# Running sums of Strassen–Winograd block products made by accumulating in a PSUM bank (SwiGLU of a two-layer encoder)

## The chip, the cores and the metric

One NeuronCore of one Trainium2 (trn2) chip. The metric is the device time of the kernel in microseconds (us): the median of three runs. Before the change it is 3169.98 us (3168.97 to 3172.48).

## What is computed

A trunk of two layers is run on two inputs, a prompt and a sample, each of 512 tokens with 1024 features. Each layer adds a self-attention, a cross-attention to a memory and a SwiGLU to the residual; a last RMS norm ends it. Cut to what matters here:

```python
D_MODEL, SEQ, DEPTH, D_FF = 1024, 512, 2, 2816

def swiglu(h, w_gu, w_down):
    g, u = jnp.split(h @ w_gu, 2, axis=-1)
    return (jax.nn.silu(g) * u) @ w_down

def trunk(x, mem, ...):
    for layer in range(DEPTH):
        x = x + mix(rms_norm(x, norm_mix[layer]))          # layer 0: GQA and differential attention, layer 1: MLA
        x = x + memory_cross_attn(rms_norm(x, norm_cross[layer]), ...)
        x = x + swiglu(rms_norm(x, norm_ffn[layer]), w_gu[layer], w_down[layer])
    return rms_norm(x, final_norm)
```

All data are fp32. The change touches only the two SwiGLUs.

## The kernel before

**Matmuls.** Activations lie transposed, features on the 128 partitions and the 512 tokens of one input along the row, so that a tile is 128x512. An fp32 product is made of three matmuls on values that are split into a high and a low part (`gemm_k`, L726 to L729): high by high (L727), high by low (L728), low by high (L729). L96 casts the high part on ACT and L97 subtracts it for the low part on DVE or POOL.

**Seven products instead of eight.** The SwiGLU treats the two inputs together. A pair of weight row blocks makes two block rows, the two inputs make two block columns, and the 2x2 block product is done by Strassen and Winograd's scheme with seven block products P1 to P7. With u2 = P1+P6 and u3 = u2+P7 the four blocks of the result are c11 = P1+P2, c12 = u2+P5+P3, c21 = u3+P4 and c22 = u3+P5. Column 1 is the prompt (b = 0), column 2 the sample (b = 1). c21 and c22 are the two inputs of the "up" half, c11 and c12 those of the gate half, in the first matrix multiply.

**Weight operands.** `lhs_ops` (L994 to L1028) loads two weight row blocks r0 and r1 (tiles `wr`, three buffers, DMAs of L998 and L999, issued by SP), splits r0 whole (tiles `wh`, `wl`, two buffers: products 1 and 2), makes four combinations (tiles `ws`, three buffers; on POOL in the first matrix multiply, on DVE in the second) and splits those: s1 is for product 5, s2 for 6, s4 for 3, s3 for 7, and r1's right half (`a`) for 4. Each of these five has one buffer. In the first matrix multiply a cast of ACT (L96) and a subtraction of DVE (L97) make each; the next pair of blocks is loaded when the combinations and subtractions that read the `wr` tile are through.

**Products and banks.** `product` (L1030 to L1039) takes its PSUM bank from a rotation pg, pss, pg, pt: three banks of pg, two of pss, two of pt (and one `pa` for small things). Each product starts its bank afresh, and each is taken out of it by one ACT copy or one DVE addition.

**gate_up** (L1124 to L1168) makes the first matrix multiply in 22 chunks, each 7 products of 12 matmuls. ACT copies P1 (L1131) and P5 (L1135) out; DVE adds P2, P6, P7, P3 and P4 to what there is (helper `tt`, so these have the line L506); POOL adds P5 to u2 and to u3, and DVE's addition of P3 reads u2 after POOL's addition. Then both columns are scaled by 1/rms (tiles R), ACT makes the SiLU (L1150), POOL multiplies, and the operands of the second multiply are formed and stored (L1159 to L1168). In the first chunk of a layer R[1] is still being made: `settle` sends a few 128x1 matmuls (L143) and a broadcast (L160) through PE between products.

**down** (L1170 to L1240) makes the second matrix multiply over four groups of k blocks (2, 3, 3, 3), in each over four row pairs q, in each over the seven products. The right operands (`u` tiles) are loaded, cast (L1205) and subtracted once in a group. Seven accumulators for each q, 28 tiles, keep the seven sums of products over the groups: in group 0 three begin as the residual and four as an ACT copy of the product (L1221), and all else is added by DVE. After the last group each q takes eight additions of accumulators (L1226 to L1235), three on POOL and five on DVE, and one more residual; then `new_x` stores it and forms the next layer's operands. In layer 1 `down_last` (L1242 to L1303) does the last group for the two columns in turn and makes the final norm.

**Order.** The program is recorded in the order of the code, and a scheduler that simulates a timeline then fixes the order of the instructions on each engine, for all engines apart. On the chip each engine executes its list in that order and waits at the head of the list. SP issues the DMAs of loads and stores in the same way.

Of the kernel before, what the change touches and what calls it, by code (L numbers as in the profile page):

```python
# [34 lines left out]
def trunk_kernel(ctx, tc, xt, memt, gains, lams, w_in0, w_out0, w_in1, w_uq, w_ukv, w_out1,  # L35
# [690 lines left out]
    def gemm_k(o, wh, wl, xh, xl, first, last):  # L726
        nc.tensor.matmul(o, lhsT=wh, rhs=xh, start=first, stop=False)  # L727
        nc.tensor.matmul(o, lhsT=wh, rhs=xl, start=False, stop=False)  # L728
        nc.tensor.matmul(o, lhsT=wl, rhs=xh, start=False, stop=last)  # L729
# [394 lines left out]
    def gate_up(l, gp, B, hd):  # L1124
        ctile = lambda: gp.tile([128, T], F32, tag="c", name=nm("c"), bufs=5)
        for c in range(NFF):
            A = lhs_ops(gp, w_gu[l, 2 * c], w_gu[l, 2 * c + 1], 512, nc.gpsimd if c else nc.vector, nc.vector)
# [3 lines left out]
            nc.scalar.copy(p1, product(1, A, B))  # L1131
# [342 lines left out]
```

## Time and profile before

| what | us |
|---|---|
| median of three runs | 3169.98 |
| the profiled execution | 3166.0 |
| its span | 3164.2 |
| PE busy in the span | 2967.1 |
| gate_up of layer 0 and its rim, about | 940 to 1404 |
| down of layer 0, about | 1404 to 1670 |
| gate_up of layer 1, about | 2400 to 2875 |
| down of layer 1, about | 2875 to 3136 |

The granted TensorE clock is 0.972 of full speed over the span. PE is TensorE's matmuls, PEld its weight loads, which overlap; DVE is VectorE, ACT ScalarE, POOL GpSimd, and SP issues DMAs. A group of the profile reads: line, engine, operation, output <- inputs, shape and count | busy us, mean ns of one | idle time just before them and what ended it. Windows of the span give the busy time and instruction count of each engine in a stretch.

### The profile page before, as it was taken

What the parts mean: (1) busy time and instruction counts of PE and PEld (TensorE: products, weight loads), DVE (VectorE), ACT (ScalarE), POOL (GpSimd) and SP (SyncE); (2) the same over time, 40 slices, a digit from 0 to 9 for tenths busy, and PEclk for the clock granted to TensorE, in tenths of its full rate; (3) what the DMA queues carried; (4) which work ended last, traced back from release to release, by engine and by line L of the source; (5) the groups of instructions that cost most, each with busy time, mean ns of one, the idle gap of its engine ahead of it and who ended that gap; (6) DMA issues with size and microseconds to landing.
All of it is one profiled execution on the core that took longest, in us unless ns stands there. A gap on an engine that the chain in (4) does not pass through costs nothing. (4 is left out here: it accounts for less than half of the span.)

```text
span 3164.2 us, 42343 instructions
## 1 busy us (share of the span) xinstructions
PE 2967.1 (94%) x14301; PEld 2438.6 (77%) x14301; DVE 2187.6 (69%) x3561; ACT 1348.0 (43%) x2554; POOL 1814.1 (57%) x1334
## 2 busy tenths in 40 slices
PE   8999999999988999988989899999997999998996
PEld 6878889878877877766767688888885888776774
DVE  7566676655587666677795566657569666668778
ACT  3255456535433232234442456656443322224432
POOL 4453445537576555657694333645667666556666
PEclk9999999999999999999999899999998999999998
DMA  4454653634342222244441777644442222225432
GB/s 145 165 172 141 217 190 131 203 103 167 123 143 74 100 100 94 97 149 149 150 148 56 238 256 242 209 148 147 147 157 90 97 95 96 91 99 190 157 128 81
DMA packets 204137, 449.70 MB, mean 142 GB/s; under 512 B 21264, under 2 KB 47248, under 8 KB 203920
## 3 DMA queue, kind: packets, MB, share of 16 engines
q1 hardware_dynamic: 203776, 446.95, 41.1%
q8 instruction: 114, 1.87, 0.2%
q14 instruction: 103, 0.84, 0.1%
q10 hardware_dynamic: 144, 0.04, 0.0%
HBM read 315.83 MB, written 131.07 MB: 141 GB/s over the span
## 5 line engine op out<-in xcount | busy, mean ns | idle before, releaser
L108 POOL TENSOR_TENSOR wl<-wr,wh 128x1024 fp32r<-128x1024 f32 (+1 forms) x160 | 396.9, 2482 | 317.5 <-ACT wh L107 312.4
L115 PE MATMUL pg<-u,wh 128*128 128x512 f32 x1360 | 546.0, 403 | 27.7 <-DVE acc L506 7.3
L117 PE MATMUL pg<-u,wl 128*128 128x512 f32 x1360 | 542.5, 399 | 11.1 <-POOL wl L108 10.8
L116 PE MATMUL pg<-u,wh 128*128 128x512 f32 x1360 | 544.4, 400 | 5.2 <-DVE u L231 4.8
L430 POOL TENSOR_SCALAR p<-p,rs 128x512 f32<-128x512 f32 (+1 forms) x288 | 194.3, 678 | 386.5 <-DVE rs L426 335.2
L115 PEld LDWEIGHTS pg<-u,wh 128*128 128x128 f32 x1360 | 260.7, 192 | 87.4 <-ACT wh L107 7.1
L117 PEld LDWEIGHTS pg<-u,wl 128*128 128x128 f32 x1360 | 260.6, 192 | 66.9 <-POOL wl L108 14.5
L116 PEld LDWEIGHTS pg<-u,wh 128*128 128x128 f32 x1360 | 260.7, 192 | 61.7 <-DVE u L231 10.9
L107 ACT CAST wh<-wr 128x1024 fp32r<-128x1024 f32 (+2 forms) x168 | 168.7, 1009 | 213.6 <-PE pg L116 146.6
L96 ACT CAST s<-ws 128x512 fp32r<-128x512 f32 (+2 forms) x304 | 165.9, 560 | 199.5 <-POOL ws L506 86.6
L727 PE MATMUL pg<-u,s 128*128 128x512 f32 x462 | 189.2, 409 | 45.9 <-DVE c L506 20.6
L425 ACT ACTIVATE p<-p,mx 128x512 f32<-128x512 f32 (+1 forms) x256 | 171.3, 670 | 102.8 <-DVE mx L422 95.3
L438 ACT CAST ptt<-pt 128x512 fp32r<-128x512 f32 (+1 forms) x288 | 151.3, 537 | 144.1 <-PE pt L436 141.2
L506 POOL TENSOR_TENSOR f<-f,c 128x512 f32<-128x512 f32 x132 | 174.2, 1321 | 63.7 <-DVE f L506 58.0
L439 DVE TENSOR_TENSOR ptt<-pt,ptt 128x512 fp32r<-128x512 f32 (+1 forms) x288 | 177.7, 624 | 40.9 <-ACT ptt L438 39.0
L1150 ACT ACTIVATE c<-c 128x512 f32<-128x512 f32 x88 | 55.7, 633 | 335.6 <-DVE c L506 335.5
L728 PE MATMUL pg<-u,s 128*128 128x512 f32 x462 | 188.0, 407 | 4.5 <-DVE u L506 4.4
L729 PE MATMUL pg<-u,s 128*128 128x512 f32 x462 | 187.7, 406 | 2.2 <-POOL s L97 2.2
L97 DVE TENSOR_TENSOR s<-ws,s 128x512 fp32r<-128x512 f32 x176 | 179.0, 1017 | 8.9 <-ACT s L96 6.8
L96 ACT CAST wh<-wr 128x1024 fp32r<-128x1024 f32 (+2 forms) x76 | 71.3, 938 | 253.2 <-DMA wr<-in_w_gu_dram 175.2
L226 POOL TENSOR_TENSOR ssq<-ssq,f 128x512 f32<-128x512 f32 x100 | 160.6, 1608 | 26.5 <-ACT f L224 26.2
L97 POOL TENSOR_TENSOR s<-ws,s 128x384 fp32r<-128x384 f32 (+1 forms) x128 | 149.3, 1176 | 38.5 <-ACT s L96 36.0
(368 smaller groups left out, 8187.2 us busy)
## 6 DMA issues: line engine op xcount, KB each, us to landing
dram<-hl SPq DMA_DIRECT2D x88, 512.0 KB, 3.1
wr<-in_w_gu_dram SPq DMA_DIRECT2D x88, 512.0 KB, 3.2
u<-dram SPq DMA_DIRECT2D x160, 256.0 KB, 4.8
dram<-f SPq DMA_DIRECT2D x152, 256.0 KB, 2.1
kk<-dram SPq DMA_DIRECT2D x52, 512.0 KB, 4.9
q<-dram SPq DMA_DIRECT2D x96, 256.0 KB, 4.1
vt<-dram SPq DMA_DIRECT2D x84, 256.0 KB, 3.1
wr<-in_w_down_dram SPq DMA_DIRECT2D x50, 384.0 KB, 3.0
```

The source lines that it names most:

```text
L96: nc.scalar.copy(hi, f)
L97: (eng or nc.vector).tensor_tensor(out=lo, in0=f, in1=raw(hi), op=SUB)
L108: (nc.vector if first else nc.gpsimd).tensor_tensor(out=l[:, cs], in0=r[:, cs], in1=raw(h[:, cs]), op=SUB)
L115: nc.tensor.matmul(ps, lhsT=wh, rhs=xh, start=(i == 0), stop=False)
L116: nc.tensor.matmul(ps, lhsT=wh, rhs=xl, start=False, stop=False)
L117: nc.tensor.matmul(ps, lhsT=wl, rhs=xh, start=False, stop=(i == n - 1))
L430: nc.gpsimd.tensor_scalar(out=p, in0=p, scalar1=rs, scalar2=1.0, op0=MUL, op1=MUL)
L439: nc.vector.tensor_tensor(out=pl, in0=tv, in1=raw(ph), op=SUB)
L506: eng.tensor_tensor(out=out, in0=a, in1=b, op=op)
L727: nc.tensor.matmul(o, lhsT=wh, rhs=xh, start=first, stop=False)
L728: nc.tensor.matmul(o, lhsT=wh, rhs=xl, start=False, stop=False)
L729: nc.tensor.matmul(o, lhsT=wl, rhs=xh, start=False, stop=last)
```

## The change

A product no longer owns a bank. A chunk (or a row pair) takes three banks: one of pg takes products 1, 6, 7, 4 one after the other, one of pss takes 5 and 3, one of pt takes 2. Only the first matmul into a bank starts it afresh; the products behind it accumulate on top. So the bank of pg shows P1, then P1+P6, then u3, then c21; whatever reads a running sum reads it between two products, and the next product into that bank waits for this reader.

In gate_up ACT copies out the bank after products 1, 6, 5 and 7 (L1144 to L1146 of the changed kernel: S1, S6, S5, S7). DVE makes c11 = P2+S1 and c12 = (P5+P3)+S6, and multiplies c21 by R[0] straight out of the bank. POOL makes c22 = S7+S5. For each chunk three DVE additions and one POOL addition are gone, and two ACT copies are new.

In down four accumulators for each q, 16 tiles, all begin as the residual (four loads for each q in group 0). DVE adds the bank to one of them after each product: after 1 and 2 to c11's, after 6 and 3 to c12's, after 4 to c21's, after 7 and 5 to c22's. For each layer the 16 ACT copies of group 0 become DVE additions, and the eight closing additions for each q (20 of DVE and 12 of POOL) and the six `u` tiles among the accumulators are gone. In layer 1 `sums` replaces the bodies of `first` and `second`.

```diff
-    def product(i, A, B):
-        ps = banks[bank[0] % 4]()
-        bank[0] += 1
+    def product(i, A, B, ps, first):
         n = len(B[i])
         for k in range(n):
             wh, wl = (x[:, k * 128:(k + 1) * 128] for x in A[i])
-            gemm_k(ps, wh, wl, *B[i][k], k == 0, k == n - 1)
+            gemm_k(ps, wh, wl, *B[i][k], first and k == 0, k == n - 1, skip_group_check=True)
         return ps
-    banks, bank = (pg, pss, pg, pt_), [0]
+    CHAIN = {1: 0, 6: 0, 7: 0, 4: 0, 5: 1, 3: 1, 2: 2}
+    class Banks:
+        def __init__(self, A, B):
+            self.A, self.B, self.ps = A, B, [None] * 3
+        def __call__(self, i):
+            j = CHAIN[i]
+            first = self.ps[j] is None
+            if first:
+                self.ps[j] = (pg, pss, pt_)[j]()
+            return product(i, self.A, self.B, self.ps[j], first)
...
-            u3 = up[1]
-            p1 = ctile()
-            nc.scalar.copy(p1, product(1, A, B))
-            g0 = ctile()
-            tt(nc.vector, g0, product(2, A, B), p1, ADD)
-            p5 = ctile()
-            nc.scalar.copy(p5, product(5, A, B))
-            settle(1, pa, rms[1], begin=True)
-            u2 = ctile()
-            tt(nc.vector, u2, product(6, A, B), p1, ADD)
-            tt(nc.vector, u3, product(7, A, B), u2, ADD)
-            settle(1, pa, rms[1])
-            tt(nc.gpsimd, u2, u2, p5, ADD)
-            g1 = ctile()
-            tt(nc.vector, g1, product(3, A, B), u2, ADD)
-            tt(nc.vector, up[0], product(4, A, B), u3, ADD)
-            tt(nc.vector, up[0], up[0], R[0], MUL)
-            tt(nc.gpsimd, u3, u3, p5, ADD)
-            tt(nc.gpsimd, up[1], u3, R[1], MUL)
-            for b, g in enumerate((g0, g1)):
-                tt(nc.vector, g, g, R[b], MUL)
-                nc.scalar.activation(g, g, AF.Silu)
-                tt(nc.gpsimd, up[b], up[b], g, MUL)
+            P, S, g = Banks(A, B), {}, [None, None]
+            def keep(i):
+                S[i] = ctile()
+                nc.scalar.copy(S[i], P(i))
+            def c11():
+                g[0] = ctile()
+                tt(nc.vector, g[0], P(2), S[1], ADD)
+            def c12():
+                tt(nc.vector, S[6], P(3), S[6], ADD)
+                g[1] = S[6]
+            def c21():
+                tt(nc.vector, up[0], P(4), R[0], MUL)
+            keep(1)
+            c11()
+            if c:
+                keep(6)
+                keep(5)
+                keep(7)
+                c12()
+            else:
+                keep(5)
+                settle(1, pa, rms[1], begin=True)
+                keep(6)
+                c12()
+                settle(1, pa, rms[1])
+                keep(7)
+            c21()
+            tt(nc.gpsimd, up[1], S[7], S[5], ADD)
+            tt(nc.gpsimd, up[1], up[1], R[1], MUL)
+            for b in range(2):
+                tt(nc.vector, g[b], g[b], R[b], MUL)
+                nc.scalar.activation(g[b], g[b], AF.Silu)
+                tt(nc.gpsimd, up[b], up[b], g[b], MUL)
...
-        spare = [u_tile(g_, k_, F32) for g_, k_ in (("B", 0), ("B", 4), (y, 4)) for _ in range(2)]
-        spare += tile_(gp, "c", 5) + tile_(f_p, "f", 5)[:1] + tile_(gp, "x", 8)
-        spare += tile_(f_p, "res", 1) + tile_(f_p, "of", 1) + tile_(f_p, "sh", 1)
-        spare += tile_(r_p, "ra", 1) + tile_(r_p, "r", 4)
-        for q in range(4):
-            acc.append(dict(zip((2, 3, 4, 1, 6, 5, 7), spare[7 * q:])))
+        tile_ = lambda p, t, n: [p.tile([128, T], F32, tag=t, name=nm("acc"), bufs=k)
+                                 for k in (n,) * min(n, 7)]
+        spare = tile_(r_p, "ra", 1) + tile_(r_p, "r", 4)[:2] + tile_(f_p, "f", 5)[:1]
+        spare += tile_(gp, "c", 5) + tile_(gp, "x", 8)
+        acc = [spare[4 * q:4 * q + 4] for q in range(4)]
+        into = {1: 0, 2: 0, 6: 1, 3: 1, 4: 2, 7: 3, 5: 3}
+        rows = lambda q: ((0, q), (1, q), (0, q + 4), (1, q + 4))
         for gi, c0 in enumerate((0, 4, 10, 16)):
             hk = 3 if gi else 2
-            order = (1, 2, 3, 5, 6, 7, 4) if gi else (1, 2, 5, 6, 3, 7, 4)
+            order = (1, 2, 6, 5, 7, 3, 4) if gi else (1, 2, 5, 6, 3, 7, 4)
...
-                    for i, b, m in ((2, 0, q), (3, 1, q), (4, 0, q + 4)):
-                        dma(a[i], res[b][m])
+                    for f, (b, m) in zip(a, rows(q)):
+                        dma(f, res[b][m])
+                P = Banks(A, B)
                 for i in order:
-                    ps = product(i, A, B)
-                    if gi == 0 and i in (1, 5, 6, 7):
-                        nc.scalar.copy(a[i], ps)
-                    else:
-                        tt(nc.vector, a[i], ps, a[i], ADD)
+                    f = a[into[i]]
+                    tt(nc.vector, f, P(i), f, ADD)
                 if not last:
                     continue
-                r22 = f_tile()
-                dma(r22, res[1][q + 4])
-                tt(nc.gpsimd, a[2], a[2], a[1], ADD)
-                tt(nc.vector, a[6], a[6], a[1], ADD)
-                tt(nc.vector, a[7], a[7], a[6], ADD)
-                tt(nc.gpsimd, a[3], a[3], a[5], ADD)
-                tt(nc.gpsimd, a[5], a[5], r22, ADD)
-                tt(nc.vector, a[3], a[3], a[6], ADD)
-                tt(nc.vector, a[4], a[4], a[7], ADD)
-                tt(nc.vector, a[5], a[5], a[7], ADD)
-                for b, m, i in ((0, q, 2), (1, q, 3), (0, q + 4, 4), (1, q + 4, 5)):
-                    out[b][m] = a[i]
-                    new_x(b, m, a[i], g_next, st[b], "AB"[b])
+                for f, (b, m) in zip(a, rows(q)):
+                    new_x(b, m, f, g_next, st[b], "AB"[b])
...
+        def sums(q, A, b, order):
+            P = Banks(A, B)
+            for i in order:
+                f = acc[q][into[i]]
+                tt(nc.vector, f, P(i), f, ADD)
+            for f, (b_, m) in zip(acc[q], rows(q)):
+                if b_ == b:
+                    st[b].add(f, nc.vector if q == 3 else None)
+                    outs[b].append((m, f))
+        first = lambda q, A: sums(q, A, 0, (1, 2, 6, 7, 4))
+        second = lambda q, A: sums(q, A, 1, (5, 3))
```

The places where the order of instructions moves, with buffer numbers in the names. First PE in the first chunk of layer 0's gate_up, before; `pa` and L143 are `settle`, and the `pg` behind it is product 5:

```order
L728 MATMUL pss_10155<-u_9529,wh_10105 128x512
L729 MATMUL pss_10155<-u_9528,wl_10106 128x512
L143 MATMUL pa_10184<-cols,ssq_9652 128x1 x4
L727 MATMUL pg_10170<-u_9659,s_10111 128x512
L728 MATMUL pg_10170<-u_9660,s_10111 128x512
L729 MATMUL pg_10170<-u_9659,s_10112 128x512
L727 MATMUL pg_10170<-x_9804,s_10111 128x512
```

The same place on PE after the change; `pg_10320` and `pt_10335` are products 1 and 2 of the second chunk:

```order
L729 MATMUL pt_10155<-u_9528,wl_10106 128x512
L727 MATMUL pg_10320<-u_9141,wh_10285 128x512
L728 MATMUL pg_10320<-u_9142,wh_10285 128x512
L727 MATMUL pt_10335<-u_9390,wh_10285 128x512
L728 MATMUL pt_10335<-u_9391,wh_10285 128x512
L143 MATMUL pa_10184<-cols,ssq_9652 128x1 x4
L729 MATMUL pg_10320<-u_9141,wl_10286 128x512
L727 MATMUL pg_10320<-u_9226,wh_10285 128x512
L728 MATMUL pg_10320<-u_9227,wh_10285 128x512
```

24 matmuls of the second chunk's products 1 and 2 have moved ahead of product 5 of the first chunk, some of them ahead of the small matmuls.

ACT over one chunk of gate_up, before; L1131 and L1135 are the copies of P1 and P5, `wh` is the cast of a newly loaded weight tile, L1150 the SiLU:

```order
L1131 COPY c_10957<-pt_10958 128x512
L96 CAST wh_11239<-wr_11235 128x1024
L1150 ACTIVATE c_10972<-c_10972 128x512
L96 CAST s_11090<-ws_11088 128x512
L1135 COPY c_10987<-pss_10988 128x512
L96 CAST s_11096<-ws_11094 128x512
L96 CAST s_11108<-ws_11106 128x512
L96 CAST s_11102<-ws_11100 128x512
L1150 ACTIVATE c_11032<-c_11032 128x512
L96 CAST a_11112<-wr_11081 128x512
```

ACT over one chunk after the change; L1146 is a copy out of a running sum (first S6, then S5, S7, and S1 of the next chunk), L1178 the SiLU:

```order
L96 CAST a_10772<-wr_10741 128x512
L96 CAST wh_11048<-wr_11044 128x1024
L96 CAST s_10905<-ws_10903 128x512
L1146 COPY c_10808<-pg_10779 128x512
L1146 COPY c_10822<-pss_10823 128x512
L1178 ACTIVATE c_10793<-c_10793 128x512
L96 CAST s_11054<-ws_11052 128x512
L96 CAST s_10917<-ws_10915 128x512
L1146 COPY c_10837<-pg_10779 128x512
L1146 COPY c_10927<-pg_10928 128x512
L96 CAST s_10911<-ws_10909 128x512
L1178 ACTIVATE c_10808<-c_10808 128x512
```

The cast of `wh` now stands three places ahead of the copy of S6, and there are four copies in place of two.

DVE over one chunk of gate_up, before; `c<-pss` is the addition of P3, `f<-pg` those of P7 and P4:

```order
L97 TENSOR_TENSOR s_11562<-ws_11559,s_11561 128x512
L506 TENSOR_TENSOR c_11479<-pt_11480,c_11434 128x512
L97 TENSOR_TENSOR s_11568<-ws_11565,s_11567 128x512
L506 TENSOR_TENSOR f_11433<-pg_11494,c_11479 128x512
L97 TENSOR_TENSOR s_11580<-ws_11577,s_11579 128x512
L506 TENSOR_TENSOR c_11509<-pss_11510,c_11479 128x512
L97 TENSOR_TENSOR s_11574<-ws_11571,s_11573 128x512
L506 TENSOR_TENSOR c_11509<-c_11509,r_10242 128x512
L506 TENSOR_TENSOR f_11432<-pg_11524,f_11433 128x512
L97 TENSOR_TENSOR a_11584<-wr_11552,a_11583 128x512
L506 TENSOR_TENSOR f_11432<-f_11432,r_9757 128x512
L506 TENSOR_TENSOR c_11604<-pg_11605,c_11589 128x512
```

DVE over one chunk after the change; `f<-pg` with `r` is c21 by R[0], `c<-pt` is c11 and `c<-pss` c12:

```order
L506 TENSOR_TENSOR f_10776<-pg_10779,r_9757 128x512
L97 TENSOR_TENSOR a_10922<-wr_10890,a_10921 128x512
L506 TENSOR_TENSOR c_10942<-pt_10943,c_10927 128x512
L97 TENSOR_TENSOR wl_11198<-wr_11193,wh_11197 128x1024
L506 TENSOR_TENSOR c_10942<-c_10942,r_9757 128x512
L97 TENSOR_TENSOR s_11061<-ws_11058,s_11060 128x512
L506 TENSOR_TENSOR t_10885<-f_10777,f_10776 128x512
L97 TENSOR_TENSOR s_11204<-ws_11201,s_11203 128x512
L97 TENSOR_TENSOR s_11073<-ws_11070,s_11072 128x512
L506 TENSOR_TENSOR c_10957<-pss_10972,c_10957 128x512
L97 TENSOR_TENSOR s_11067<-ws_11064,s_11066 128x512
L506 TENSOR_TENSOR c_10957<-c_10957,r_10240 128x512
```

Three reads of banks are left of five, and none of them has an input that POOL makes.

More of the change, by code (lines that the diff above doesn't have):

```diff
@@ L724, in attn_diff, with gemm_k @@
             new_o(of, grp, os_)
[L726 to L729, printed above, removed]
+    def gemm_k(o, wh, wl, xh, xl, first, last, **k):
+        nc.tensor.matmul(o, lhsT=wh, rhs=xh, start=first, stop=False, **k)
+        nc.tensor.matmul(o, lhsT=wh, rhs=xl, start=False, stop=False, **k)
+        nc.tensor.matmul(o, lhsT=wl, rhs=xh, start=False, stop=last, **k)
     sqn = [[dram([128, 2, T]) for _ in range(8)] for _ in range(2)]
@@ L1170, in down @@
     def down(l, gp, x, y, hd, g_next):
-        out = [[None] * KC, [None] * KC]
-        acc = []
         st = [Stats(), Stats()]
-        tile_ = lambda p, t, n: [p.tile([128, T], F32, tag=t, name=nm("acc"), bufs=n)
-                                 for _ in range(n)]
-        spare = [u_tile(g_, k_, F32) for g_, k_ in (("B", 0), ("B", 4), (y, 4)) for _ in range(2)]
-        spare += tile_(gp, "c", 5) + tile_(f_p, "f", 5)[:1] + tile_(gp, "x", 8)
-        spare += tile_(f_p, "res", 1) + tile_(f_p, "of", 1) + tile_(f_p, "sh", 1)
-        spare += tile_(r_p, "ra", 1) + tile_(r_p, "r", 4)
-        for q in range(4):
-            acc.append(dict(zip((2, 3, 4, 1, 6, 5, 7), spare[7 * q:])))
+        tile_ = lambda p, t, n: [p.tile([128, T], F32, tag=t, name=nm("acc"), bufs=k)
[5 more added lines that the diff above has]
+        rows = lambda q: ((0, q), (1, q), (0, q + 4), (1, q + 4))
         for gi, c0 in enumerate((0, 4, 10, 16)):
             hk = 3 if gi else 2
-            order = (1, 2, 3, 5, 6, 7, 4) if gi else (1, 2, 5, 6, 3, 7, 4)
+            order = (1, 2, 6, 5, 7, 3, 4) if gi else (1, 2, 5, 6, 3, 7, 4)
             last = gi == 3
@@ L1207, in down @@
             if last and g_next is None:
-                return down_last(l, gp, B, acc, st)
+                return down_last(l, gp, B, acc, into, rows, st)
             for q in range(4):
@@ L1257, in down_last @@
         outs = [[], []]
-        def add_to(i, q, A):
-            tt(nc.vector, acc[q][i], product(i, A, B), acc[q][i], ADD)
-        def first(q, A):
-            a = acc[q]
-            r22 = f_tile()
-            dma(r22, res[1][q + 4])
-            for i in (1, 2, 6, 7, 4):
-                add_to(i, q, A)
-            tt(nc.vector, a[2], a[2], a[1], ADD)
-            tt(nc.vector, a[6], a[6], a[1], ADD)
-            tt(nc.vector, a[7], a[7], a[6], ADD)
-            tt(nc.vector, a[4], a[4], a[7], ADD)
-            for m, i in ((q, 2), (q + 4, 4)):
-                st[0].add(a[i], nc.vector if q == 3 else None)
-                outs[0].append((m, a[i]))
-            tt(nc.gpsimd, a[7], a[7], r22, ADD)
-            tt(nc.gpsimd, a[3], a[3], a[6], ADD)
-        def second(q, A):
-            a = acc[q]
-            add_to(5, q, A)
-            tt(nc.vector, a[3], a[3], a[5], ADD)
-            tt(nc.vector, a[5], a[5], a[7], ADD)
-            add_to(3, q, A)
-            for m, i in ((q + 4, 5), (q, 3)):
-                st[1].add(a[i], nc.vector if q == 3 else None)
-                outs[1].append((m, a[i]))
+        def sums(q, A, b, order):
[9 more added lines that the diff above has]
+        second = lambda q, A: sums(q, A, 1, (5, 3))
         ops = lambda q, *want: lhs_ops(gp, *src(q), nc.vector, nc.gpsimd, *want)
```

2 lines of the change are left out of this document (1 added, 1 removed).

## The prediction

> **What bounds the kernel now.** I read the page first: which engine is full, and over the whole span. The two lines are the span and the busy times of the engines.
>
> ```profile
> span 3164.2 us, 42343 instructions
> PE 2967.1 (94%) x14301; PEld 2438.6 (77%) x14301; DVE 2187.6 (69%) x3561; ACT 1348.0 (43%) x2554; POOL 1814.1 (57%) x1334
> ```
>
> PE is busy for 94%, and the change removes no matmul. All it can win is PE's idle time in the two SwiGLUs, or the rim of the span. So the next view is the windows, stage by stage: length, then busy time and instructions of PE, PEld, DVE, ACT and POOL, granted clock, DMA share, GB/s.
>
> ```profile
> 940.00:964.00 24.00, 11.03 (x40) 8.59 (x38) 23.93 (x27) 10.37 (x16) 18.70 (x11) 0.75 0.14 51
> 964.00:1160.00 196.00, 196.00 (x839) 158.44 (x840) 131.74 (x162) 59.03 (x99) 116.47 (x86) 0.99 0.26 95
> 1160.00:1404.00 244.00, 233.13 (x998) 186.09 (x998) 162.24 (x195) 70.31 (x120) 143.63 (x106) 1.00 0.27 98
> 2446.00:2700.00 254.00, 253.35 (x1097) 204.88 (x1096) 171.44 (x200) 75.28 (x126) 155.92 (x114) 1.00 0.27 97
> 2700.00:2875.00 175.00, 168.18 (x714) 134.30 (x713) 116.89 (x139) 50.27 (x86) 102.90 (x77) 0.99 0.27 95
> 1404.00:1500.00 96.00, 79.52 (x309) 59.50 (x309) 76.47 (x93) 45.60 (x93) 65.82 (x53) 0.95 0.52 183
> 1500.00:1600.00 100.00, 95.63 (x404) 75.60 (x403) 78.49 (x98) 44.66 (x81) 63.73 (x48) 0.98 0.46 158
> 1600.00:1652.00 52.00, 47.61 (x194) 36.99 (x192) 48.54 (x48) 20.18 (x35) 52.00 (x35) 0.96 0.36 119
> 1652.00:1670.00 18.00, 13.18 (x36) 8.97 (x37) 18.00 (x18) 4.33 (x7) 14.93 (x9) 0.69 0.33 117
> 2875.00:2970.00 95.00, 80.44 (x300) 59.74 (x300) 74.59 (x91) 45.97 (x93) 67.10 (x54) 0.91 0.53 185
> 2970.00:3070.00 100.00, 95.80 (x404) 76.24 (x402) 72.37 (x92) 42.83 (x77) 61.14 (x47) 0.98 0.48 162
> 3070.00:3136.00 66.00, 55.90 (x228) 42.04 (x227) 60.95 (x69) 17.90 (x33) 54.59 (x38) 0.97 0.12 43
> ```
>
> The second row has no idle time at all: 196 / 839 = 0.2336 us per matmul, so a chunk of 84 matmuls can't go below 19.6 us. Here PE is the bound. In the rows behind it, a few per cent are idle; around group 0 of down (from 1404 and 2875) it is 15 to 17%. What ends these waits is in PE's rows of the timeline (start, length, engine, line, tiles, and in brackets the idle time and its releaser), two out of each gate_up and two of down, with the two starts ahead of them:
>
> ```profile
> 963.87 0.79 PE L727 MATMUL pg<-u,s 128*128 128x512 f32 x1 [9.70 <-ACT s L96]
> 2438.34 0.80 PE L727 MATMUL pg<-u,s 128*128 128x512 f32 x1 [10.32 <-ACT s L96]
> 1168.09 0.47 PE L727 MATMUL pg<-u,s 128*128 128x512 f32 x1 [1.16 <-DVE c L506]
> 1372.43 0.47 PE L727 MATMUL pg<-u,s 128*128 128x512 f32 x1 [2.00 <-DVE c L506]
> 1475.59 0.50 PE L728 MATMUL pss<-u,s 128*128 128x512 f32 x1 [3.05 <-DVE u L506]
> 2890.44 0.65 PE L728 MATMUL pt<-u,s 128*128 128x512 f32 x1 [3.21 <-DVE u L506]
> ```
>
> Between the third and fourth row lie ten chunks: (1372.43 - 1168.09) / 10 = 20.43 us for each, 0.8 us over the floor. PE waits for a bank that DVE hasn't emptied, and DVE in turn waits, as the groups of 1000 to 1390 us show (busy, mean ns | idle before, releaser):
>
> ```profile
> L506 DVE TENSOR_TENSOR c<-pg,c 128x512 f32<-128x512 f32 x28 | 19.2, 685 | 43.4 <-POOL c L506 43.4
> L506 DVE TENSOR_TENSOR c<-pt,c 128x512 f32<-128x512 f32 x15 | 10.3, 684 | 5.9 <-POOL c L506 5.9
> L506 POOL TENSOR_TENSOR c<-c,c 128x512 f32<-128x512 f32 x19 | 27.1, 1428 | 11.7 <-ACT s L96 11.7
> ```
>
> DVE's addition of P3 stands behind POOL's u2 + P5 (1.43 us, at the end of a queue of combinations). That is the one link of gate_up in which work, not PE, sets the time.
>
> **The change in gate_up.** This link goes: P5 + P3 is summed in the bank, and no read of a bank has an input of POOL's. DVE loses three additions of 0.685 us, POOL one of 1.43 us, and ACT gains two copies, a duration that the DMA fence below shows as 0.58 us. None is full (DVE 67%, ACT 30%, POOL 59% of 1160 to 1404), so the counts themselves cost or win nothing; the link does. PE idles 244.00 - 233.13 = 10.9 us there, 0.65 in 2446 to 2700 and 6.8 in 2700 to 2875, together 18.3. I take 15.5 and leave 2.8 for new waits; bounds 0 (the ring of weights keeps the pace, rival A) and 18.3. That the new waits are small is a choice: between two products of one bank the order puts other work, 24 matmuls between 6 and 7 and between 7 and 4, or 24 x 0.2336 = 5.6 us in which the reader must finish.
>
> The start: PE stands still for 9.70 and 10.32 us in front of product 5 of the first chunk. There 24 matmuls of the second chunk now come first, 5.6 us. Less 2 us for new short waits (the broadcast of the norm now stands right behind product 6), 3.6 for each layer, 7.2 in all; bounds 0 and 11.2.
>
> **The change in down.** In group 0 sixteen ACT copies become DVE additions. The first row prices them; the other two show what the merging of accumulators costs in 1400 to 1660 us.
>
> ```profile
> L506 DVE TENSOR_TENSOR acc<-pg,acc 128x512 f32<-128x512 f32 x32 | 21.8, 680 | 2.7 <-PE pg L729 2.5
> L506 DVE TENSOR_TENSOR acc<-acc,acc 128x512 f32<-128x512 f32 x10 | 15.5, 1559 | 0.2
> L506 POOL TENSOR_TENSOR acc<-acc,acc 128x512 f32<-128x512 f32 x5 | 7.2, 1446 | 0.0
> ```
>
> 16 x 0.68 = 10.9 us more on a DVE that is busy 80% there (76.47 of 96) and that PE waits for (the last two rows of the timeline). Against that, down's products 1 and 2 of q = 0 now stand ahead of product 7 of chunk 20, the next group's first products stand in the group before, and six of the accumulators no longer occupy operand tiles. Fully exposed it costs 2 x 10.9 = 22; at best it wins most of the idle 16.5 + 14.6 = 31, say 28. I take a gain of 6, a little above the middle, since DVE's idle third of late gate_up lies next to it.
>
> Groups 1 to 3 up to the last few: PE idles 4.4 + 4.4 and 4.2 + 10.1 = 23 us. Where the last group ends, DVE is 93% and POOL 100% busy (1600 to 1652), and the closing additions, 20 x 1.56 = 31 us of DVE and 12 x 1.45 = 17 us of POOL a layer, leave it. DVE's share spreads over four q, most of it covered by PE. I take 10; bounds 0 and 19. The way out of layer 0 (1652 to 1670) has DVE at 18.00 of 18.00 and PE idle for 4.8 at a clock of 0.69: I take 4, bounds 0 and 8.
>
> The end: the last matmul is followed by the last additions and the norm.
>
> ```profile
> 3135.29 0.39 PE L729 MATMUL pt<-u,s 128*128 128x512 f32 x1
> 3137.54 0.68 DVE L506 TENSOR_TENSOR acc<-pt,acc 128x512 f32<-128x512 f32 x1
> 3138.14 0.15 DVE L123 TENSOR_SCALAR v<-pa 128x4 f32<-128x4 f32 x1
> ```
>
> The last product ends at 3135.68 and is taken up only at 3137.54, since DVE is still merging. 1.86 us can go; I take 1.3, bounds 0 and 1.9. The four residual loads for each q (before three, and one later) are hoisted into gate_up, where the DMAs are busy a quarter of the time: nothing.
>
> Sum: 15.5 + 7.2 + 6 + 10 + 4 + 1.3 = 44. From the profiled execution's 3166.0 this is 3122; the median of the runs is 4 higher, so 3169.98 - 44 = 3126.
>
> **Rivals.** A: the weight ring holds gate_up. Without PE the timeline of one chunk shows the ring's turn:
>
> ```profile
> 1108.70 0.61 ACT L96 CAST a<-wr 128x512 fp32r<-128x512 f32 x1
> 1109.21 0.58 ACT L1131 COPY c<-pss 128x512 f32<-128x512 f32 x1
> 1109.34 1.70 DVE L97 TENSOR_TENSOR a<-wr,a 128x512 fp32r<-128x512 f32 x1 [0.67 <-ACT a L96]
> 1111.06 0.33 SPq L998 DMA_DIRECT2D wr<-in_w_gu_dram  x1
> 1114.21 1.05 ACT L96 CAST wh<-wr 128x1024 fp32r<-128x1024 f32 x1 [4.42 <-DMA wr<-in_w_gu_dram]
> ```
>
> The subtraction that reads r1 ends at 1111.04, the load is sent at 1111.06, and ACT waits for it until 1114.21: 5.5 us from cast to cast. If this turn, and not POOL's addition, makes the 20.43 us, gate_up keeps its idle time: 3126 + 15.5 = 3142. Against it: the recorded wait is POOL's, 43.4 us of DVE; for it: the loads now wait for combinations of POOL's that have moved.
>
> B: group 0 is bound by DVE at full price, -22 in place of +6: 3126 + 28 = 3154. For it are the rows of waits for `u`; against it the slack on both sides.
>
> C, the slow side: the links show. In a chain the next product of a bank may not begin until the copy is out, and ACT runs in order. The copy of S6 now stands behind the cast of `wh`, which waits for a DMA. The cover is 5.6 us from product 6 to 7; with 0.58 for the copy the cast must end within 5.0 us behind product 6. If it ends later, PE stops, and the stop delays the operands that release the next load, so it comes again in each chunk: 44 us for each us late. With all four reads of a chunk exposed, 4 x 0.58 x 44 chunks = 102 us and nothing won in gate_up: 3126 + 15.5 + 102 = 3244. For it is the row of 4.42 us above; against it, by the order I reckon the cast done about 4 us ahead of need.
>
> The row of 0.58 us beside a cover of 5.6 says that the reader hides. [...]
>
> D: the additions were hidden anyway and nothing moves: 3170.
>
> **How the numbers follow.** Forecast 0.66, A 0.13, B 0.09, C 0.10, D 0.02. The predicted time is the forecast's, 3126. With every gain at its upper bound, 18.3 + 11.2 + 28 + 19 + 8 + 1.9 = 86, it would be 3084; all at once is unlikely, so the low end is 3090. The high end takes in A and B: 3156. About 0.2% of the time, 6.3 us, can be told from no change. Faster: the forecast, A, and 0.05 of B, which by its price lies 16 us below the time before, 0.84. Same: the other 0.04 of B, should A's loss come on top, and D, 0.06. Slower: C, 0.10.
>
> **What would show it.** Right: a gate_up without idle time, 19.6 us a chunk; no wait of DVE for POOL ahead of a read of a bank; about 4 to 6 us of stop at the start; fewer waits for `u` about group 0; the last group with DVE under 90%; the last addition right behind the last matmul. Wrong: PE waiting for the copies of L1146 (C), or for `wh` or its low part (A), or a longer stretch of group 0 with DVE full (B).

## The result and the profile after

The changed kernel takes 3087.8 us (median of four runs, 3084.74 to 3092.32) beside 3171.23 for the kernel before (3168.97 to 3176.46): a ratio of 0.9739, 95% interval 0.9723 to 0.9755. The forecast was 3126, range 3090 to 3156. The direction is right, the gain of 83 us is almost twice the 44 forecast, and the time lies 2 us under the range.

The page of the changed kernel, as before: span, then busy time, share and instructions of each engine.

```profile
span 3083.0 us, 41876 instructions
PE 2942.8 (95%) x14301; PEld 2429.3 (79%) x14301; DVE 2065.6 (67%) x3417; ACT 1391.7 (45%) x2610; POOL 1785.5 (58%) x1270
```

PE executes the same 14301 matmuls; the span is 81.2 us shorter, but its busy time also falls by 24 us. Where the 81.2 us lie can be counted without windows of fixed times: each layer's SwiGLU has 2772 matmuls, and it is cut alike in both traces behind the first 168 (two chunks), 1764 (21 chunks), 2016 (end of group 0 of down), 2268 and 2520 of them and at the start of the last one. Times in us, both layers summed:

| stretch | before | after | gain | forecast |
|---|---|---|---|---|
| start, two chunks | 118.0 | 104.6 | 13.4 | 7.2 |
| steady gate_up, 19 chunks | 759.1 | 740.4 | 18.7 | 15.5 |
| chunk 21 to the end of group 0 | 153.3 | 136.0 | 17.3 | 6 |
| groups 1 and 2 | 258.2 | 247.9 | 10.3 | 10 (groups 1 to 3) |
| group 3 | 146.7 | 128.8 | 17.9 | |
| layer 0's end to layer 1's gate_up | 758.7 | 754.3 | 4.4 | 4 |
| last matmul to the end | 28.9 | 29.3 | -0.4 | 1.3 |

(The stretch ahead of the first gate_up is 0.4 longer.) Now the windows that show these stretches after; columns as in the prediction.

```profile
994.00:1364.00 370.00, 370.00 (x1597) 299.07 (x1596) 230.65 (x252) 143.08 (x236) 241.23 (x153) 1.00 0.29 106
1364.00:1432.00 68.00, 62.46 (x255) 47.62 (x254) 64.59 (x85) 31.32 (x64) 49.24 (x40) 0.97 0.67 228
1432.00:1556.00 124.00, 120.50 (x507) 96.32 (x506) 89.26 (x120) 48.21 (x87) 77.84 (x60) 0.97 0.42 136
1556.00:1624.00 68.00, 63.86 (x268) 51.06 (x267) 52.97 (x60) 33.05 (x60) 55.33 (x40) 0.97 0.45 154
2431.00:2801.00 370.00, 370.00 (x1597) 299.07 (x1596) 232.90 (x252) 143.43 (x236) 241.81 (x153) 1.00 0.30 106
2994.00:3054.00 60.00, 58.81 (x251) 46.50 (x249) 38.53 (x50) 21.42 (x41) 42.42 (x34) 1.00 0.22 70
```

Steady gate_up has no idle time in either layer, and a chunk takes 370.2 / 19 = 19.5 us. DVE's share of the last group of layer 1 is 64% (38.53 of 60). Only the way into down (second row) is still tight: DVE 64.59 of 68.

The reads of the banks in the changed gate_up, groups of 1000 to 1390 us (busy, mean ns | idle before, releaser):

```profile
L1146 ACT COPY c<-pg 128x512 f32<-128x512 f32 x61 | 33.5, 583 | 0.0
L506 DVE TENSOR_TENSOR c<-pss,c 128x512 f32<-128x512 f32 x20 | 13.8, 691 | 29.3 <-PE pss L729 29.3
L506 DVE TENSOR_TENSOR f<-pg,r 128x512 f32<-128x512 f32 x20 | 13.8, 690 | 58.1 <-PE pg L729 58.1
L727 PE MATMUL pg<-u,a 128*128 128x512 f32 x61 | 24.2, 397 | 0.6 <-ACT c L1146 0.6
```

DVE now waits for PE and no longer for POOL. The last row answers the fear of rival C: PE waits once, 0.6 us, for an ACT copy between two products of a bank, and in the whole run there is no other such wait. In down the links do show, over the whole run:

```profile
PE pg L727 <- DVE acc L506: 11.8, 12, 2.8
PE pss L727 <- DVE acc L506: 2.0, 2, 1.6
```

### The profile page after: what moved, and what is told of

Same layout as the page of the kernel before. It is cut to its first block, busy times and chain, and to the rows that moved or that the text cites. A ratio compares the mean times of both kernels' runs of the same rounds, so it can differ in the third digit from the quotient of the medians.

```text
span 3083.0 us, 41876 instructions
## 1 busy us (share of the span) xinstructions
PE 2942.8 (95%) x14301; PEld 2429.3 (79%) x14301; DVE 2065.6 (67%) x3417; ACT 1391.7 (45%) x2610; POOL 1785.5 (58%) x1270
## 5 line engine op out<-in xcount | busy, mean ns | idle before, releaser
L107 ACT CAST wh<-wr 128x1024 fp32r<-128x1024 f32 (+2 forms) x168 | 168.7, 1009 | 214.9 <-PE pg L116 145.8
L727 PE MATMUL pss<-u,s 128*128 128x512 f32 x484 | 192.2, 398 | 7.2 <-ACT s L96 4.6
L506 POOL TENSOR_TENSOR f<-f,c 128x512 f32<-128x512 f32 x88 | 149.1, 1695 | 79.0 <-DVE f L506 75.8
L729 PE MATMUL pss<-u,s 128*128 128x512 f32 x484 | 192.3, 397 | 0.7 <-DVE s L97 0.7
L728 PE MATMUL pss<-u,s 128*128 128x512 f32 x484 | 192.1, 397 | 0.0
L727 PE MATMUL pg<-u,s 128*128 128x512 f32 x440 | 175.5, 399 | 5.0 <-DVE acc L506 2.7
L728 PE MATMUL pg<-u,s 128*128 128x512 f32 x440 | 174.5, 397 | 2.0 <-DVE u L506 2.0
```

Of the source, the lines that this page charges most:

```text
L729: nc.tensor.matmul(o, lhsT=wl, rhs=xh, start=False, stop=last, **k)
```

## The experiments

Theory at the outset: the parts of the gain belong to the places where the table has them, and in gate_up the wait of DVE for POOL is the cause. Rivals: the gain about group 0 comes out of gate_up; the wait only stands in the record, and the number of bank reads or the way in which the banks are shared matters. Each kernel was timed beside the one before on the same chip.

**One half alone.** The changed gate_up with the old down, and the old gate_up with the changed down; only whole functions are exchanged.

> The changed gate_up with the down of before (seven accumulators, rotating banks). Counted from the trace, the gain of 81 us in the span is 18.6 in steady gate_up, 13.5 at its start, 17.4 from chunk 21 to the end of group 0, 28 in groups 1 to 3 and 4.4 on the way out of layer 0. Theory 1, the parts add up and each belongs to its own function: 32 us of 81, so about 3139 beside 3171 for before. Theory 2, the gain about group 0 comes from gate_up's banks, which let down's first products start early: 32 + 17 = 49 us, about 3122.

> The gate_up of before with the changed down (four accumulators, banks that accumulate). Theory 1: 17.4 + 28 + 4.4 = 50 us gained, about 3121. Theory 2, the gain about group 0 needs the changed gate_up: 32 us, about 3139. Rival B of the prediction, sixteen more DVE additions in group 0 cost about 10 us a layer and the gain there comes from elsewhere: about 3130 or more.

Measured 3117.86 (ratio 0.9824, 0.9800 to 0.9849) and 3140.54 (0.9902, 0.9882 to 0.9922), beside 3171.11. gate_up alone gives 53 us, down alone 31, and 53 + 31 = 84 is the whole: the halves add up. But the cut is theory 2's. With the changed gate_up alone the stretch into down takes 63.4 and 63.2 us (before 76.6 and 76.7); with the changed down alone 76.5 and 80.8. What I had put down to down is gate_up's.

**One word.** In the kernel before, DVE in place of POOL adds P5 to u2:

```diff
-            tt(nc.gpsimd, u2, u2, p5, ADD)
+            tt(nc.vector, u2, u2, p5, ADD)
```

> Before, with one word changed: u2 + P5 is added by DVE and not by POOL. No accumulation in a bank. Theory: DVE's wait for POOL ahead of P3 makes steady gate_up slow, so its 18 us go and the rest stays: 3153, with chunks of 19.5 us. Rival: it is the number of bank reads, or the weight ring behind them, and the wait for POOL only stands in the record: chunks stay at 20.4 us and the time within 5 us of 3171, or above, since DVE has 0.7 to 1.6 us more to do in a chunk.

Measured 3124.22 (0.9855, 0.9835 to 0.9874): 47 us, where 18 were expected. Steady gate_up takes 369.1 us in each layer (before 380.6 and 378.5), and the way into down 65.3 in each, as good as the changed kernel or better. So this one addition is worth 21 us in the steady part and 23 behind it. The windows show it, first this kernel's two stretches:

```profile
1001.00:1370.00 369.00, 369.00 (x1597) 299.23 (x1596) 284.94 (x323) 116.76 (x190) 214.93 (x153) 1.00 0.29 102
1370.00:1436.00 66.00, 61.80 (x257) 48.54 (x256) 52.09 (x69) 31.21 (x66) 39.76 (x33) 0.97 0.62 210
```

then before, the same two, and a piece out of the second:

```profile
1000.00:1381.00 381.00, 371.80 (x1600) 298.85 (x1599) 249.62 (x296) 110.44 (x186) 229.16 (x170) 1.00 0.27 96
1381.00:1457.00 76.00, 63.87 (x252) 49.18 (x251) 61.11 (x77) 33.68 (x70) 45.44 (x38) 0.93 0.56 198
1410.00:1425.00 15.00, 10.82 (x31) 8.03 (x30) 15.00 (x20) 10.81 (x22) 10.07 (x8) 0.68 0.65 236
```

In the steady part DVE does more work here than before (284.94 beside 249.62 us) and PE has no gap: DVE's load was not what held PE there. The last row is where the price grows: 31 matmuls in 15 us at a granted clock of 0.68. PE's timeline of before at this place:

```profile
1409.32 0.76 PE L727 MATMUL pg<-u,s 128*128 128x512 f32 x1 [2.70 <-DVE c L506]
1409.88 0.63 PE L728 MATMUL pg<-u,s 128*128 128x512 f32 x1
...
1413.89 0.50 PE L727 MATMUL pss<-u,s 128*128 128x512 f32 x1 [0.71 <-ACT u L1205]
1417.85 0.79 PE L728 MATMUL pss<-u,s 128*128 128x512 f32 x1 [3.46 <-DVE u L506]
```

The wait of 2.70 us was ended by DVE's addition of product 6 of the last chunk. DVE and POOL at this place:

```profile
1407.88 0.69 DVE L506 TENSOR_TENSOR u<-u,u 128x512 fp32r<-128x512 f32 x1 [0.99 <-ACT u L1205]
1408.49 0.68 DVE L506 TENSOR_TENSOR c<-pg,c 128x512 f32<-128x512 f32 x1
1412.05 1.66 POOL L506 TENSOR_TENSOR c<-c,c 128x512 f32<-128x512 f32 x1
```

DVE's addition stands behind the subtraction of an operand of down, which had waited for its cast; POOL's addition of this chunk runs only later, so PE didn't wait for it here. The wait of 3.46 us is for an operand of down itself. After each of the two, matmuls follow at 0.43 us in place of 0.23. That the 23 us hang on the one addition is shown by this run, and by e13 below; by which waits they do is not shown.

**The link put back, and taken apart.** In the changed kernel product 3 gets its own bank and POOL adds S5 to S6 (e10). In the kernel before POOL's addition stays on POOL but writes to the tile of the sum, so that it needn't wait until product 7's addition has read u2 (e13); or product 4 comes ahead of product 3 (e17).

```diff
 e10
+                tt(nc.gpsimd, S[6], S[6], S[5], ADD)
+                P.ps[1] = None
                 c12()
...
 e13
+            g1 = ctile()
+            tt(nc.gpsimd, g1, u2, p5, ADD)
             tt(nc.vector, u3, product(7, A, B), u2, ADD)
...
-            tt(nc.gpsimd, u2, u2, p5, ADD)
-            g1 = ctile()
-            tt(nc.vector, g1, product(3, A, B), u2, ADD)
+            tt(nc.vector, g1, product(3, A, B), g1, ADD)
 e17
-            tt(nc.vector, g1, product(3, A, B), u2, ADD)
             tt(nc.vector, up[0], product(4, A, B), u3, ADD)
+            tt(nc.vector, g1, product(3, A, B), u2, ADD)
```

> The changed kernel with the link through POOL put back in gate_up: product 3 gets a bank of its own, POOL adds S5 to S6, and DVE adds the result to P3; products 1, 6, 7, 4 still share a bank. Theory: this link alone set the pace of gate_up and delayed the way into down, so steady gate_up takes 380 us a layer again (+18 in two) and the stretch from chunk 21 to the end of group 0 loses 8 to 11 us a layer: 3088 + 34 to 40 = 3122 to 3128. Rival: fewer bank reads by DVE are what helps, and these stay fewer: 3088 to 3095.

> Before, with POOL still adding u2 and P5 and DVE still adding P3 to the result, but POOL writes into the tile of the sum to come instead of over u2, so that it may begin as soon as product 6 is added and need not wait until product 7's addition has read u2. Theory, it is the late start: the gain of the kernel with this addition on DVE comes back, 3124 to 3130, with steady gate_up at 369 to 371 us. Rival, any trip over POOL's queue of combinations between two additions of DVE is too long: 3150 to 3171.

> Before, with product 4 ahead of product 3 in gate_up, nothing else: POOL's addition still begins after product 7, but twelve matmuls, 2.8 us, now stand ahead of product 3. Theory, the addition is too late by less than that: 3124 to 3135. Rival, the delay is not in the time between 7 and 3 but in POOL's queue as a whole: 3160 to 3171.

e10: 3095.64 (0.9753, 0.9738 to 0.9767). My theory falls: with an addition of POOL's ahead of product 3, steady gate_up stays at 369.5 and 369.2 us; only the way into down loses 5.1 and 3.9. e13: 3124.88 beside 3177.90 (0.9840, 0.9819 to 0.9861), the same as with DVE, steady 369.1 in both layers and the way into down 63.6 and 65.5. e17: 3152.95 (0.9925, 0.9903 to 0.9946), between its two forecasts: steady 369.6 and 369.1, but the way into down rises to 82.0 and 82.3. The group rows, e13 and e17 in 1000 to 1340 us:

```profile
L506 POOL TENSOR_TENSOR c<-c,c 128x512 f32<-128x512 f32 x18 | 31.3, 1741 | 0.0
L506 DVE TENSOR_TENSOR c<-pg,c 128x512 f32<-128x512 f32 x26 | 17.9, 687 | 10.2 <-PE pg L729 10.2
```

```profile
L506 POOL TENSOR_TENSOR c<-c,c 128x512 f32<-128x512 f32 x17 | 22.2, 1307 | 1.3 <-ACT a L96 1.3
L506 DVE TENSOR_TENSOR c<-pg,c 128x512 f32<-128x512 f32 x24 | 16.5, 689 | 28.3 <-POOL c L506 18.0 <-POOL f L506 9.0 <-ACT c L1131 1.3
```

In e13 POOL's addition is even longer (1.74 us beside 1.43) and DVE's addition of P3 doesn't wait for it, so POOL's speed is not the cause. What held the addition stands in the rows of POOL and DVE. Before, a chunk that costs nothing, and the next one, in which PE then waits 2.00 us (1372.43):

```profile
1347.20 1.59 POOL L506 TENSOR_TENSOR c<-c,c 128x512 f32<-128x512 f32 x1 [1.29 <-ACT s L96]
1348.83 0.69 DVE L506 TENSOR_TENSOR c<-pt,c 128x512 f32<-128x512 f32 x1 [1.17 <-POOL c L506]
```

```profile
1365.51 0.68 DVE L506 TENSOR_TENSOR f<-pss,c 128x512 f32<-128x512 f32 x1
1369.05 1.29 POOL L506 TENSOR_TENSOR ws<-wr 128x512 f32<-128x512 f32 x1 [4.01 <-DMA wr<-in_w_gu_dram]
1370.30 1.26 POOL L506 TENSOR_TENSOR c<-c,c 128x512 f32<-128x512 f32 x1
1371.59 0.69 DVE L506 TENSOR_TENSOR c<-pg,c 128x512 f32<-128x512 f32 x1 [4.80 <-POOL c L506]
```

and a chunk of e13:

```profile
1348.45 1.75 POOL L506 TENSOR_TENSOR c<-c,c 128x512 f32<-128x512 f32 x1
1351.86 1.30 POOL L506 TENSOR_TENSOR ws<-wr 128x512 f32<-128x512 f32 x1 [1.67 <-DMA wr<-in_w_gu_dram]
```

In the second chunk product 7 was added by 1366.19 and u2 could be overwritten, but in POOL's list a combination (`ws<-wr`) stands ahead of the addition and waits 4.01 us for its weight block. The addition runs 4.1 us late, and DVE stands still for 4.80. Every second chunk of 1000 to 1390 us is like this: ten times the combination waits 3.3 to 4.0 us, and DVE's ten waits behind it, 4.1 to 4.8 each, add up to the 43.4 us of the group row. In the nine chunks between them the addition starts 0.14 to 0.17 us after that of product 7 (in the first fence DVE's ended at 1347.06, and the cast that the bracket names at 1347.08), and PE never waits; all its six waits for DVE here, from 1168.09 to 1372.43, lie behind late ones.

So in the steady part the cause is the addition's place in POOL's list, behind a load. e3 takes the addition out of this list, and e13 has it ahead of the combination. In e17 it is as late as before, 3.5 to 4.5 us in 17 of the 18 chunks of 1000 to 1365 us, but twelve more matmuls cover it. In e10 it stands behind the combination, which never waits there (in 1000 to 1340 us).

The write over u2 is there in the chunks between too and costs PE nothing; whether it is why the scheduler put the addition behind the combination isn't shown, as e13 changes the tile and the place together. The longer way into down in e17 isn't explained: its longest waits of PE there, 2.44 and 2.35 us in layer 0, are for additions of DVE's that come ahead of POOL's.

**No accumulation in gate_up.** The one word of e3 together with the changed down:

> The gate_up of before with its one addition u2 + P5 on DVE, and the changed down: no accumulation over products in gate_up at all. By segments: the start without the 24 matmuls costs 12 to 13 us more than the changed kernel, steady gate_up 2 us less, the rest as in the changed one or 0 to 4 us less: 3088 + 6 to 11 = 3094 to 3099. Rival: the chained banks are needed for the way into down or for DVE's load: over 3108.

Measured 3090.03 (0.9736, 0.9717 to 0.9754), beside 0.9739 for the change: the two can't be told apart. Accumulating in the bank is worth nothing in steady gate_up beyond the late addition that it removes (738.2 us in two layers beside 740.4). At the start this kernel, without the 24 matmuls in the stop, takes 12.4 us more; besides the 2.2 here it wins 5.2 from layer 0's end to layer 1's gate_up and 2.5 in groups 1 and 2, places where nothing of gate_up stands.

**The start.** `with tc.issue_after(...)` holds products 1 and 2 of the second chunk behind the first matmul of product 5 of the first (the lines that set `head` are left out):

```diff
+            with tc.issue_after(head[5].ins) if c == 1 else ExitStack():
+                keep(1)
+                c11()
```

> The changed kernel with products 1 and 2 of the second chunk held behind the first matmul of product 5 of the first, so that nothing fills the stop at the start of gate_up. Theory: the 24 matmuls placed there are the whole gain of the start, 13.5 us in two layers, so 3088 + 11 to 14 = 3099 to 3102. Rival: the stop itself is shorter for another reason (operands of product 5 ready sooner), and holding costs 0 to 4 us: 3088 to 3092.

Measured 3089.98 (0.9745, 0.9728 to 0.9763). Theory and rival were both half right. At its place the hoist is worth all of it: the start takes 58.3 and 59.2 us without it, 52.3 with it, and PE waits 10.3 us for the cast again. But the stretch from layer 0's end to layer 1's gate_up is 745.5 us in this kernel and 754.3 in the changed one, which gives 8.8 back; there PE's order of instructions differs though no line of that stage does (more on this in the last section).

**down.** The accumulators in operand tiles again (e5), the new order of products alone (e6), the closing additions put back (e7) or left out (e14), the sixteen reads of group 0 moved to DVE (e8). e14 leaves the eight additions out, so its blocks are incomplete; e7 has as many additions on the same engines, but from one of the four accumulators to the next, so its results are others too. The edits in `down_last` are left out here:

```diff
 e5
-        spare = tile_(r_p, "ra", 1) + tile_(r_p, "r", 4)[:2] + tile_(f_p, "f", 5)[:1]
-        spare += tile_(gp, "c", 5) + tile_(gp, "x", 8)
+        spare = [u_tile(g_, k_, F32) for g_, k_ in (("B", 0), ("B", 4), (y, 4)) for _ in range(2)]
+        spare += tile_(gp, "c", 5)[:4] + tile_(gp, "x", 8)[:6]
 e6, in before
-            order = (1, 2, 3, 5, 6, 7, 4) if gi else (1, 2, 5, 6, 3, 7, 4)
+            order = (1, 2, 6, 5, 7, 3, 4) if gi else (1, 2, 5, 6, 3, 7, 4)
 e7
+                for e, j in zip("pvvppvvv", (0, 1, 3, 1, 3, 1, 2, 3)):
+                    tt(nc.gpsimd if e == "p" else nc.vector, a[j], a[j], a[j - 1], ADD)
 e14, in before
-                tt(nc.gpsimd, a[2], a[2], a[1], ADD)
...
-                tt(nc.vector, a[5], a[5], a[7], ADD)
 e8, in before
-                        nc.scalar.copy(a[i], ps)
+                        nc.vector.tensor_copy(a[i], ps)
```

> The changed kernel with six of the sixteen accumulators in operand tiles again (two each of B0, B4 and the tail of the other group), as before had them. Theory 1: what the four accumulators free is room for the next operands, and it is worth a good part of the 28 us of groups 1 to 3: 3088 + 8 to 15 = 3096 to 3103. Theory 2: operands come in time either way: 3088 to 3092.

> Before, with the order of products in groups 1 to 3 of down as the change has it (1, 2, 6, 5, 7, 3, 4), nothing else. If the order in which operands are wanted makes the gain of groups 1 and 2 (4.2 and 5.9 us), it appears here: 3171 - 10 = 3161. If it is the additions, 3171 within 4 us.

> The changed kernel with eight additions of accumulators put back at the end of each row pair, on the engines that had them before; they add one accumulator to another, so the output isn't the reference's. Theory: the closing additions are the 18 us of group 3 and the 4 on the way out of layer 0, so 3088 + 18 to 22 = 3106 to 3110, most of it in layer 1. Rival: group 3 gains by the chained banks or the order, and the additions fit into DVE's and POOL's free time: 3088 to 3093.

> Before, without the eight closing additions of each row pair, which are left out, so the sums and the output aren't the reference's. Theory: they are most of the gain of group 3 (18 us) and of the way out of layer 0 (9 us by its first 40 matmuls): 3171 - 22 to 27 = 3144 to 3149. Rival: it is the order of the last group or the residual load in it: 3165 or more.

> Before, with the four ACT copies of each row pair of group 0 made by DVE: the price of 16 more bank reads a layer on DVE by itself. Rival B of the prediction: all exposed, 2 x 16 x 0.68 = 22 us, 3193. From the runs so far (chunk 21 to the end of group 0 takes 63.3 us with the down of before and 68 with the changed one, gate_up changed in both): 4 to 5 us a layer, 3171 + 9 = 3180. Hidden: 3171 to 3174.

Beside 3173.08 for the kernel before (e14: 3171.41), with 258.2 and 146.7 in the last two columns:

| | us | ratio | interval | groups 1, 2 | group 3 |
|---|---|---|---|---|---|
| e5 | 3092.36 | 0.9743 | 0.9726 to 0.9761 | 256.3 | 127.9 |
| e6 | 3180.09 | 1.0022 | 1.0010 to 1.0033 | 266.6 | 149.8 |
| e7 | 3123.85 | 0.9846 | 0.9830 to 0.9863 | 251.0 | 152.9 |
| e14 | 3143.66 | 0.9904 | 0.9889 to 0.9919 | 262.8 | 123.2 |
| e8 | 3170.58 | 0.9989 | 0.9979 to 0.9998 | 255.7 | 144.1 |

The closing additions are shown from both sides. Leaving them out takes 27.8 us off before; putting them back adds 36 to the changed kernel (34 by the ratios), more than the 18 to 22 expected, perhaps because each adds to the result of the one ahead of it (not shown). In e7 group 3 takes 24 us more, and the stretch from layer 0's end to layer 1's gate_up 16 more. Group 3 of layer 0, before, after, and with the additions put back:

```profile
1585.00:1657.00 72.00, 64.90 (x255) 49.88 (x254) 68.54 (x69) 31.84 (x55) 67.73 (x45) 0.93 0.42 144
```

```profile
1556.00:1624.00 68.00, 63.86 (x268) 51.06 (x267) 52.97 (x60) 33.05 (x60) 55.33 (x40) 0.97 0.45 154
```

```profile
1560.00:1634.00 74.00, 66.40 (x267) 51.51 (x265) 68.14 (x69) 29.35 (x52) 69.09 (x46) 0.95 0.38 126
```

DVE goes from 95% to 78% and back to 92%, POOL from 94% to 81% and back to 93%. The operand tiles carry 8.4 of the 10.3 us of groups 1 and 2 at their place, though the whole time rises by only 4.6 (the change's interval and this one overlap). The order alone loses 7 us. The sixteen reads on DVE cost 4.4 us on the way into down, and groups 1 to 3 win 5.1 back; in sum nothing, so rival B's price wasn't there.

**Two attempts to do better.** In group 0 four reads of each row pair are ACT copies again, and the residual is added by POOL in group 1 (e12); group 0 has the order of the other groups (e15).

```diff
 e12
+                if gi == 1:
+                    for f, t, (b, m) in zip(a, ("of", "sh", "res", "f"), rows(q)):
...
+                        tt(nc.gpsimd, f, f, r, ADD)
...
+                    if gi == 0 and i in (1, 5, 6, 4):
+                        nc.scalar.copy(f, P(i))
 e15
-            order = (1, 2, 6, 5, 7, 3, 4) if gi else (1, 2, 5, 6, 3, 7, 4)
+            order = (1, 2, 6, 5, 7, 3, 4)
```

> The changed kernel, but in group 0 of down four of the seven reads of each row pair are ACT copies again that begin the four accumulators, and the residual is loaded in group 1 and added by POOL. If DVE's sixteen additions cost 4 us a layer on the way into down (68 us beside 63.3 with the down of before) and POOL's sixteen in group 1 lie in its free time: 3088 - 8 = 3080. Rival: POOL, 63% busy there and the maker of the low parts of the weights, becomes late: 3088 or more.

> The changed kernel with the order 1, 2, 6, 5, 7, 3, 4 in group 0 of down too, where products 7 and 4 of one bank follow one another at present. If the waits for a bank's reader (11.8 us in 12 waits in down) matter there: 3088 - 2 to 4 = 3084 to 3086. If the order in which group 0's operands arrive matters more: 3090 or more.

Measured 3108.65 (0.9795, 0.9778 to 0.9812) and 3089.61 (0.9729, 0.9708 to 0.9749). e12 misses: the way into down becomes 3.8 and 2.9 us longer in place of shorter, and group 1 takes 70.2 and 72.4 beside 65.3 and 65.2, where POOL has sixteen more additions. e15 can't be told from the change. No kernel here beats it clearly.

## Why the prediction was right in sign and wrong in size

**What failed.** Two steps. The first is the step in down's group 0, "I take a gain of 6, a little above the middle": measured 17.3 to its end. It was priced as down's own affair, sixteen DVE additions against better cover. The runs show that it hangs on gate_up's link: one word in gate_up gives 22.7 us there (e13 24.2), the changed down alone nothing (157.3 us beside 153.3), and the sixteen reads by themselves cost 4.4. Through which waits the link works there stays open.

The second is the size of groups 1 to 3, "I take 10; bounds 0 and 19": measured 28.2, over the bound. The mechanism was right (the closing additions, by e7 and e14; the freed operand tiles, by e5), but the bound wasn't one. I took PE's loss as the length less the busy time. In the row of 3070 to 3136 that is 66 - 55.90 = 10.1; by count, 228 matmuls at 0.2336 us are 53.3, and 12.7 are lost. In the row of 2875 to 2970 it is 14.6 against 95 - 300 x 0.2336 = 24.9. Where the clock was down, matmuls were busy and late: over 1417.8 to 1424 us of before, at a granted clock of 0.59, PE is busy for 6.15 of 6.20 us with 17 matmuls, 4.0 us by count. Nor were the rows the stages: group 0 ends at 1457.5 and 2930.0, so the rows to 1500 and 2970 that I took for group 0 hold some 40 us of group 1 each, and the first 23 and 22 us of the last chunk stood in the rows of gate_up. The two terms together, 16, measured 45.5. The busy time of PE fell by 24 us for the same matmuls: that part of the gain I could not have seen in any idle time.

**Steady gate_up** (15.5; measured 18.7, the upper bound 18.3): right, and the link named was the right one, "at the end of a queue of combinations" included. What it missed is why the queue was late in every second chunk: the combination ahead waited up to 4.0 us for its load. POOL's addition cost the steady part nothing where that combination came behind it (e13, 369.1 us in both layers) or found its block loaded (e10, 369.5 and 369.2). I had read the releaser of DVE's wait, but not what POOL's addition itself had stood behind.

**The start** (7.2; measured 13.4, over the upper bound 11.2): the mechanism is right by e4. The timeline after shows the 24 matmuls inside the stop, with product 5 after them no later than before (963.36 beside 963.87 at starts of gate_up 0.4 us apart):

```profile
951.98 1.05 PE L143 MATMUL pa<-cols,ssq 128*128 128x1 f32 x8 [1.07 <-POOL ssq L226]
954.75 0.80 PE L729 MATMUL pg<-u,wl 128*128 128x512 f32 x1 [1.72 <-DVE wl L97]
963.36 0.50 PE L727 MATMUL pss<-u,s 128*128 128x512 f32 x1 [2.33 <-ACT s L96]
```

The waits that I subtracted lie within the old stop and cost nothing more, and the clock over the two chunks (the third number from the end) is 0.86 before and 0.93 after:

```profile
941.00:1000.00 59.00, 46.03 (x182) 36.38 (x181) 48.53 (x62) 22.00 (x36) 38.68 (x25) 0.86 0.17 61
```

```profile
942.00:994.00 52.00, 44.09 (x181) 34.59 (x180) 39.19 (x50) 20.97 (x34) 33.79 (x23) 0.93 0.19 66
```

**The way out of layer 0** (4; measured 4.4): right only by number. Counted to its 40th matmul it gains 9.6 us (8.7 beside 18.3), and loses 5 of them in layer 1's attention, where PE's order differs from before.

**The end** (1.3; measured -0.4). After the change, the last matmul and the first short operation of the two norms:

```profile
3053.70 0.40 PE L729 MATMUL pss<-u,s 128*128 128x512 f32 x1
3055.38 0.16 DVE L123 TENSOR_SCALAR v<-pa 128x4 f32<-128x4 f32 x1 [0.56 <-PE pa L143]
3067.65 0.15 DVE L123 TENSOR_SCALAR v<-pa 128x4 f32<-128x4 f32 x1
```

The first starts 3055.38 - 3054.10 = 1.3 us behind the last matmul in place of 2.5, close to the forecast. The second starts 12.3 us behind the first, before 10.8 (3138.14 and 3148.91), and that gives it back.

**Rivals.** A fell as a bound: chunks go at 19.5 us, with the same ring also in e3, where POOL waits 59 us for weight blocks in 1000 to 1340 us and PE not at all. But a load of this ring is part of the wait that I put to POOL alone. B fell by e8. C fell: one wait of 0.6 us in gate_up, 13.8 us in down, over two layers, already inside the gain. This case's bubbles, one every second chunk, went with the same banks and buffers in e13; they meant one addition behind a load. That load was sent at 1365.06, right behind the end of the combination ahead of it (1365.04), so more buffers for weights might have done it too; no run tries that.

One correction: "20 of DVE and 12 of POOL" closing additions is layer 0's count; in layer 1 the code has 24 and 8.

## What to carry to other kernels

Bound a gain in TensorE's time by the count of matmuls times the best cadence that the trace shows, not by idle time, and where a stretch runs at a lower clock look first at the wait ahead of it (here waits of 2.70 and 3.46 us, with matmuls 0.43 us apart behind them). Where an engine waits for another's operation, ask what that operation stood behind in its own engine's list: here it was a load that it didn't need, and a fresh tile for the sum, with which the addition came ahead of it, took some 50 us off this kernel without a faster engine. Ask of a large rewrite which one line of it could do the same: here one word did more than half.
